# Where the low part of a weight tile is made: a VectorE subtraction, or an accumulating transfer onto a negated copy

## The chip, the cores and the metric

The kernel runs on one core of one Trainium2 chip. Its time is the device time of one execution in microseconds (us); the number that counts is the median of several runs. A profiled execution gives the trace that the views below are taken from.

## What is computed

A decoder trunk of one layer on 1024 positions of 1024 channels, in float32:

```
h  = layer_norm(x)
u  = h @ w_in                        # GLU | z | x,B,C | dt | gate_a | gate_b
ya = silu(layer_norm(conv31(a * sigmoid(g)))) @ w_conv_out
yb = rms_norm(ssd(silu(conv4(xBC)), dt) * silu(z)) @ w_ssm_out
h  = layer_norm(alpha*h + (sigmoid(gate_a)*ya + sigmoid(gate_b)*yb) @ w_o)
h  = layer_norm(alpha*h + (silu(gate) * val) @ w_down),  gate,val = conv3(h @ w_up)
```

`conv31`, `conv4` and `conv3` are causal depthwise convolutions along the positions, `ssd` the chunked Mamba-2 recurrence with 32 heads in 4 groups.

## The kernel before, in words

**Two parts per operand.** The big products are done in float32r, to which a float32 number is rounded. To keep accuracy each operand is held as two float32r parts: a high part, the rounded number, and a low part, what the rounding left. A product is then three matmuls, high by high, high by low and low by high (`mm3`, L158 to L163; the last, L163, is the first to read the low part of its first operand). Activations are split by `split_to`, `transpose_to`, `split_pair` and `parts`; weights by `weights` (L144 to L153), which the change touches.

**A weight tile.** `weights` loads 128 rows of 1024 float32 numbers (512 KB) from memory into a staging tile `st` (pool `wst`, 3 buffers) through SP's queue, L147. It then takes a tile `w` of two halves of 1024 from the pool `wsp` (3 buffers; the last two tiles of each `w_down` pass come from buffers of their own). ScalarE copies `st` into the high half and rounds in doing so (L149, shown as CAST). VectorE writes `st` minus the high half into the low half (L150). For the three tiles of `first_columns` in the first half, GpSimd does that subtraction (`eng=G`). All of it is issued at a raised priority (`high_priority(offset=4000)`), so that the scheduler places it early. 284 weight tiles go through this function.

**The stages.** The positions are worked in two halves of 512. For each half: `ln_in` (normalise, transpose to `hT`), `mixers` (the in-projection, column block by column block with `column`, `z_gate` and `glu`, 24 matmuls of 512 columns for each weight tile; among them the SSD of four groups, the convolutions, and from group 2 on the first half of the SSM out-projection), `combine` (gates, second half of the SSM out-projection, the conformer's layer norm and out-projection) and the out-projection by `w_o`. For the first half that is `out_proj`; for the second it is `out_proj_pairs`, which goes through the positions in two pairs of blocks, so that every one of its 16 weight tiles serves only 12 matmuls.

Then comes the FFN. `up_first` (one weight tile `w_ue`, 24 matmuls) runs for 8 blocks ahead and then between the blocks of `up_rest`, which makes three more split tiles for each block by `split_pair` (VectorE still subtracts there; two of the three, of 1024 columns, sit in `wsp` too). `down` goes through the 22 blocks of `w_down` twice, once for each half of the positions, 24 matmuls for each weight tile.

**What sets the order.** Each engine runs its instructions in one fixed order that the scheduler wrote; an instruction that waits for a semaphore holds up all that stand behind it on its engine. SP issues every transfer of the kernel before. GpSimd has little to do: a product `au` for every chunk of the SSD (L473), the sums for the mean and the variance in `combine` (L611 to L624), a few subtractions. VectorE carries the long convolution `conv31` (L415, 480 instructions at lowered priority, fitted in where there is room), the short one (L370), the SSD's elementwise work, and the splits.

A `w` buffer is free again when the last matmul of its old tile has run. Then the high half can be written, then the low half, and then the first L163 of the new tile can run.

Of the kernel before, what the change touches and what calls it, by code (L numbers as in the profile page):

```python
# [8 lines left out]
F32 = mybir.dt.float32  # L9
F32R = mybir.dt.float32r  # L10
AF = mybir.ActivationFunctionType
ALU = mybir.AluOpType
# [43 lines left out]
def kernel(  # L56
# [15 lines left out]
    V, A, G, TE, SY = nc.vector, nc.scalar, nc.gpsimd, nc.tensor, nc.sync  # L72
# [14 lines left out]
    def bank(which):  # L87
# [20 lines left out]
        out=head_of,  # L108
        in_=ident.rearrange("p (g k h) -> p g h k", k=4, h=8),
        axis=AX.X,  # L110
        op=ALU.add,
# [3 lines left out]
        out=kind, in_=ident.rearrange("p (g k h) -> p k g h", k=4, h=8), axis=AX.XY, op=ALU.add  # L115
# [28 lines left out]
    def weights(src, name, pl=None, eng=None, bufs=None):  # L144
        with tc.high_priority(offset=4000):
            st = wst.tile([P, D], F32, tag="st", name=f"st_{name}")
            SY.dma_start(st, src)  # L147
            w = (pl or wsp).tile([P, 2, D], F32R, tag="w", bufs=bufs, name=f"w_{name}")
            A.copy(w[:, 0, :], st)  # L149
            (eng or V).tensor_tensor(  # L150
                out=w[:, 1, :], in0=st, in1=w[:, 0, :].bitcast(F32), op=ALU.subtract
            )
        return w  # L153

    def big_tile(name):
# [182 lines left out]
    def column(hh, hT, ct):  # L338
        ps = bank(1)
        project(ps, weights(wcol[ct], f"c{hh}_{ct}"), hT)  # L340
        return ps

    def first_columns(hh, hT, cts):

        ws = [weights(wcol[ct], f"c{hh}_{ct}", eng=None if hh else G) for ct in cts]
        pss = [bank(1) for _ in cts]
        for q in range(2):
            ts = slice(q * 256, (q + 1) * 256)
            for w, ps in zip(ws, pss):
                for n, (i, j) in enumerate(((0, 0), (1, 0), (0, 1))):  # L350
                    for k in range(KD):
                        TE.matmul(  # L352
                            ps[:, ts],
                            w[:, i, k * P : (k + 1) * P],
                            hT[:, j, k, ts],
                            start=n == 0 and k == 0,
                            stop=n == 2 and k == KD - 1,
                        )
        return pss
# [23 lines left out]
    def glu(pl, hh, hT, i):  # L383
        pa, pg = bank(1), bank(1)
        wa = weights(wcol[CT_A + i], f"ga{hh}_{i}")
        project(pa, wa, hT)
        wg = weights(wcol[CT_G + i], f"gg{hh}_{i}")
        project(pg, wg, hT)
        v = pl.tile([P, HALF + KC - 1], F32, tag="v", bufs=4, name=f"v{hh}_{i}")
        s = pl.tile([P, HALF], F32, tag="sig", name=f"sig{hh}_{i}")  # L390
        A.activation(out=s, in_=pg, func=AF.Sigmoid)
        A.copy(v[:, : KC - 1], v_halo[:, i, :])
        V.tensor_mul(v[:, KC - 1 :], pa, s)
        if hh == 0:
            A.copy(v_halo[:, i, :], v[:, HALF:])
        return v
# [678 lines left out]
```

## Time and profile before

| | |
|---|---|
| median of 3 runs | 2039.45 us (2036.19 to 2040.29) |
| the profiled execution: device time | 2041.08 us |
| its span in the trace | 2039.3 us |
| TensorE (PE) busy | 2000.0 us, 98% |
| VectorE (DVE) busy | 1654.7 us, 81% |
| ScalarE (ACT) busy | 973.0 us, 48% |
| GpSimd (POOL) busy | 148.0 us, 7% |
| DMA queue of SP | 278.24 MB, 40.3% of the 16 engines' span |

How to read the views: "busy" is the time in which an engine ran at least one instruction. Matmuls overlap in the record (one lasts about 390 ns, the next starts after about 227), so that PE's pace is read from the starts, or from the count in a stretch, and not from the mean. The view of groups gives, for one line of the kernel and one shape, the count, the busy time, the mean of one in ns, and the idle time before them. The view of waits says which instruction stood idle for which other one. The view of windows gives the busy time and count of each engine in a stretch, then the granted TensorE clock, the mean busy share of the 16 DMA engines, and GB/s. In the list of transfers stand the count, the size of one, and the median time from issue to landing.

### The profile page before, as it was taken

How to read it: one execution, taken by the hardware profiler on the slowest of the kernel's cores; microseconds unless marked ns; L12 is line 12 of the kernel's file. 1: busy time of each engine (PE TensorE's matmuls, PEld its weight loads, DVE VectorE, ACT ScalarE, POOL GpSimd, SP SyncE). 2: the span in 40 equal slices, each digit the busy share in tenths (PEclk: the TensorE clock that was granted, in tenths of full speed). 3: DMA queues.
4: the chain of work that ended last, by engine and by line, in shares of the span. 5: the costliest groups of instructions: out<-in, count | busy, mean ns of one | idle time of the engine just before them, and what ended most of it. 6: DMA issues, size and time to landing. Idle time of an engine off the chain costs nothing.

```text
span 2039.3 us, 24778 instructions
## 1 busy us (share of the span) xinstructions
PE 2000.0 (98%) x9296; PEld 1650.1 (81%) x9296; DVE 1654.7 (81%) x2185; ACT 973.0 (48%) x1392; POOL 148.0 (7%) x125
## 2 busy tenths in 40 slices
PE   7999999999999999999999999999999999999998
PEld 6888887888788888888888888877888888888886
DVE  7599999989766869999998976586888888853736
ACT  4465654556453356665454635354444444433231
POOL 2010101001400000100100130010000000000000
PEclk9999999999999999999999999999999999999999
DMA  6222223333436522222323353566454444464542
GB/s 218 93 69 88 86 94 104 99 103 114 158 121 213 209 88 77 90 84 76 126 88 104 109 171 128 195 217 217 155 164 157 164 165 156 160 227 149 209 159 83
DMA packets 95015, 279.81 MB, mean 137 GB/s; under 512 B 10800, under 2 KB 10800, under 8 KB 94896
## 3 DMA queue, kind: packets, MB, share of 16 engines
q1 hardware_dynamic: 94896, 278.24, 40.3%
q8 instruction: 73, 1.20, 0.2%
q14 instruction: 46, 0.38, 0.1%
HBM read 229.96 MB, written 48.23 MB: 136 GB/s over the span
## 4 chain that ended last, share of the span: by engine, by line
PE 69%; DVE 23%; issue 4%; DMA 2%; ACT 1%; SPq 0%; POOL 0%; DVEq 0%; ACTq 0%
PE acc L163 15%; PE acc L161 15%; PE acc L162 15%; DVE c L415 8%; PE sm L161 6%; PE sm L163 6%; PE sm L162 6%; DVE xbc L370 2%; PE acc L352 1%; PE sm L529 1%; PE sm L510 1%; DVE w_so L150 1%; DVE w_z L150 1%; DVE w_c L150 1%; PE sm L187 1%
## 5 line engine op out<-in xcount | busy, mean ns | idle before, releaser
L415 DVE SCALAR_TENSOR_TENSOR c<-v,pc,c 128x512 f32<-128x512 f32 x480 | 375.3, 805 | 7.2 <-ACT c L404 5.8
L473 POOL TENSOR_TENSOR au<-seg_mv,head_of 128x1024 fp32r<-128x1024 f32 x32 | 77.6, 2425 | 961.8 <-PE sm L482 728.8
L161 PE MATMUL acc<-hT,w_c 128*128 128x512 f32 x352 | 141.0, 400 | 0.0
L162 PE MATMUL acc<-hT,w_c 128*128 128x512 f32 x352 | 140.6, 399 | 0.0
L163 PE MATMUL acc<-hT,w_c 128*128 128x512 f32 x352 | 138.4, 393 | 0.0
L150 DVE TENSOR_TENSOR w_dn<-st_dn,w_dn 128x1024 fp32r<-128x1024 f32 x44 | 53.4, 1222 | 104.2 <-ACT w_dn L149 104.2
L370 DVE SCALAR_TENSOR_TENSOR xbc<-u,pc,xbc 128x512 f32<-128x512 f32 x144 | 109.8, 774 | 0.7 <-ACT xbc L368 0.5
L161 PE MATMUL sm<-h1s,w_s 128*128 128x512 f32 x264 | 103.5, 392 | 6.0 <-DVE fuv L848 3.1
L149 ACT CAST w_dn<-st_dn 128x1024 fp32r<-128x1024 f32 x44 | 46.0, 1053 | 131.6 <-PE sm L163 115.4
L162 PE MATMUL sm<-h1s,w_s 128*128 128x512 f32 x264 | 102.8, 389 | 0.0
L163 PE MATMUL sm<-h1s,w_s 128*128 128x512 f32 x264 | 102.1, 389 | 0.0
L162 PE MATMUL acc<-w_z,hT 128*128 128x512 f32 x256 | 100.8, 394 | 0.0
L161 PE MATMUL acc<-w_z,hT 128*128 128x512 f32 x256 | 100.8, 401 | 0.0
L163 PE MATMUL acc<-w_z,hT 128*128 128x512 f32 x256 | 100.7, 396 | 0.0
L149 ACT CAST w_c<-st_c 128x1024 fp32r<-128x1024 f32 x50 | 52.5, 1051 | 86.9 <-PE acc L163 66.2
L162 PEld LDWEIGHTS acc<-hT,w_c 128*128 128x128 f32 x352 | 66.1, 188 | 16.9 <-issue 3.8
L163 PEld LDWEIGHTS acc<-hT,w_c 128*128 128x128 f32 x352 | 66.1, 188 | 16.1 <-issue 2.6
L161 PEld LDWEIGHTS acc<-hT,w_c 128*128 128x128 f32 x352 | 66.1, 188 | 15.9 <-issue 2.6
L150 DVE TENSOR_TENSOR w_c<-st_c,w_c 128x1024 fp32r<-128x1024 f32 x47 | 60.6, 1289 | 20.2 <-ACT w_c L149 20.2
L163 PE MATMUL acc<-h1b,w_ue 128*128 128x512 f32 x176 | 68.5, 391 | 2.0 <-DVE w_ue L150 2.0
L161 PE MATMUL acc<-h1b,w_ue 128*128 128x512 f32 x176 | 68.7, 391 | 1.1 <-ACT s L807 0.7
L163 PE MATMUL sm<-h1b,w_s 128*128 128x512 f32 x176 | 69.2, 393 | 0.0
(312 smaller groups left out, 5741.8 us busy)
## 6 DMA issues: line engine op xcount, KB each, us to landing
st_c<-wcol SPq DMA_DIRECT2D x50, 512.0 KB, 3.5
st_dn<-wdown SPq DMA_DIRECT2D x44, 512.0 KB, 3.6
st_z<-wz SPq DMA_DIRECT2D x32, 512.0 KB, 3.4
st_wo<-wo SPq DMA_DIRECT2D x24, 512.0 KB, 3.9
st_ue<-wup SPq DMA_DIRECT2D x22, 512.0 KB, 4.1
ra<-wup SPq DMA_DIRECT2D x22, 512.0 KB, 3.8
rb<-wup SPq DMA_DIRECT2D x22, 512.0 KB, 3.5
act_scr<-fo SPq DMA_DIRECT2D x22, 512.0 KB, 2.7
```

Source lines behind the costliest of these rows:

```text
L149: A.copy(w[:, 0, :], st)
L150: (eng or V).tensor_tensor(out=w[:, 1, :], in0=st, in1=w[:, 0, :].bitcast(F32), op=ALU.subtract)
L161: TE.matmul(ps, wa(0), xa(0), start=start, stop=False, skip_group_check=more)
L162: TE.matmul(ps, wa(0), xa(1), start=False, stop=False, skip_group_check=more)
L163: TE.matmul(ps, wa(1), xa(0), start=False, stop=stop, skip_group_check=more)
L187: TE.transpose(pt[:, i * P : (i + 1) * P], src[:, (q + i) * P : (q + i + 1) * P], ident)
L352: TE.matmul(ps[:, ts], w[:, i, k * P : (k + 1) * P], hT[:, j, k, ts], start=n == 0 and k == 0, stop=n == 2 and k == KD - 1,)
L370: V.scalar_tensor_tensor(out=o, in0=u[:, k : k + HALF], scalar=pc[:, wc + k : wc + k + 1], in1=o, op0=ALU.mult, op1=ALU.add,)
L415: V.scalar_tensor_tensor(out=accs[i], in0=v[:, k : k + HALF], scalar=pc[:, wc + k : wc + k + 1], in1=accs[i], op0=ALU.mult, op1=ALU.add,)
L473: G.tensor_tensor(out=au, in0=seg_mv[:, c, :].unsqueeze(1).to_broadcast([P, 8, P]), in1=head_of[:, g, :].unsqueeze(2).to_broadcast([P, 8, P]),
L510: TE.matmul(po, CT[:, cs], S, start=True, stop=True)
L529: TE.matmul(py[:, hs], m[:, h, :], xs[:, hs], start=True, stop=True)
```

## The change

The high half is made as before. The low half is first set to the negated high half by ScalarE; then a transfer issued by GpSimd reads the same 512 KB of weights from memory a second time and adds them to what stands there. VectorE (and, for the first three tiles, GpSimd) no longer subtracts. The argument `eng` of `weights` stays but is not used any more. `st` is now read by one instruction instead of two.

```diff
@@ weights(src, name, pl=None, eng=None, bufs=None) @@
             SY.dma_start(st, src)
             w = (pl or wsp).tile([P, 2, D], F32R, tag="w", bufs=bufs, name=f"w_{name}")
             A.copy(w[:, 0, :], st)
-            (eng or V).tensor_tensor(
-                out=w[:, 1, :], in0=st, in1=w[:, 0, :].bitcast(F32), op=ALU.subtract
-            )
+            A.activation(out=w[:, 1, :], in_=w[:, 0, :].bitcast(F32), func=AF.Copy, scale=-1.0)
+            G.dma_start(w[:, 1, :], src, accum_op=ALU.add)
         return w
```

## The prediction

> **What bounds the kernel now.** I read the page first (span, busy times, queues), then who TensorE waits for, then windows of single stages, and last the groups and transfers that the change touches.
>
> ```profile
> span 2039.3 us, 24778 instructions
> PE 2000.0 (98%) x9296; PEld 1650.1 (81%) x9296; DVE 1654.7 (81%) x2185; ACT 973.0 (48%) x1392; POOL 148.0 (7%) x125
> q1 hardware_dynamic: 94896, 278.24, 40.3%
> ```
>
> TensorE has only 2039.3 - 2000.0 = 39.3 us without work. That is an outer limit for any gain that leaves the matmuls alone. Who causes those gaps is in TensorE's own waits (us in total, times, longest):
>
> ```profile
> PE sm L187 <- DVE x L225: 13.1, 3, 12.0
> PE sm L161 <- DVE fuv L848: 3.1, 4, 0.8
> PE sm L161 <- ACT w_s L726: 2.9, 2, 2.7
> PE acc L162 <- DVE yT L194: 2.9, 1, 2.9
> PE acc L163 <- DVE w_ue L150: 2.0, 2, 1.1
> PE sm L482 <- DVE state L525: 1.4, 2, 0.9
> PE acc L161 <- ACT w_wo L149: 1.1, 1, 1.1
> ```
>
> The largest, 13.1, is the layer norm before the first matmul, which the change does not shorten. The waits for VectorE after that come to 3.1 + 2.9 + 2.0 + 1.4 = 9.4 us, and only 2.0 of them are for the subtraction that goes. So VectorE, 81% busy and often in the chain of waits, hardly ever lets TensorE stand; the weight tiles arrive in time.
>
> The windows show the margins by stage (busy and count of PE, PEld, DVE, ACT, POOL; clock; DMA share; GB/s): the start, mixers, the paired out-projection, the lead of the FFN, and down:
>
> ```profile
> 0.00:50.00 50.00, 37.16 (x229) 34.33 (x230) 38.85 (x64) 23.18 (x45) 10.85 (x15) 1.00 0.65 222
> 100.00:200.00 100.00, 100.00 (x482) 81.99 (x481) 99.38 (x136) 62.63 (x102) 9.41 (x4) 1.00 0.25 83
> 1305.00:1356.00 51.00, 49.89 (x244) 41.17 (x242) 35.33 (x44) 27.51 (x39) 1.84 (x1) 1.00 0.77 272
> 1360.00:1410.00 50.00, 44.39 (x199) 35.46 (x199) 39.30 (x53) 27.25 (x45) 7.70 (x8) 1.00 0.68 232
> 1800.00:1900.00 100.00, 100.00 (x443) 82.81 (x442) 42.17 (x47) 32.12 (x39) 0.00 (x0) 1.00 0.51 181
> ```
>
> In the last row 443 matmuls take 100 us: 0.226 us each, 5.42 us for a weight tile of 24, 2.71 for one of 12. In the mixers VectorE is full, and TensorE is full as well.
>
> **The change part by part.** For each of 284 tiles:
>
> ```profile
> L149 ACT CAST w_dn<-st_dn 128x1024 fp32r<-128x1024 f32 x44 | 46.0, 1053 | 131.6 <-PE sm L163 115.4 <-DMA st_dn<-wdown 16.3
> L150 DVE TENSOR_TENSOR w_dn<-st_dn,w_dn 128x1024 fp32r<-128x1024 f32 x44 | 53.4, 1222 | 104.2 <-ACT w_dn L149 104.2
> L859 ACT ACTIVATE fo<-fug,pc 128x1024 f32<-128x1024 f32 x22 | 25.2, 1145 | 0.0
> L473 POOL TENSOR_TENSOR au<-seg_mv,head_of 128x1024 fp32r<-128x1024 f32 x32 | 77.6, 2425 | 961.8 <-PE sm L482 728.8 <-DVE seg_mv L323 232.9
> st_c<-wcol SPq DMA_DIRECT2D x50, 512.0 KB, 3.5
> r<-h_scr SPq DMA_DIRECT2D x12, 512.0 KB, 9.3
> 1820.41 0.33 SPq L147 DMA_DIRECT2D st_dn<-wdown  x1
> ```
>
> *Removed:* 281 VectorE subtractions of 1.22 us, 343 us of VectorE (and three on GpSimd). For TensorE that is worth what TensorE waited: at most 9.4 us; I take 5.
>
> *Added on ScalarE:* 284 negations. The nearest row is a scaled ACTIVATE of the same shape, 1.15 us: 326 us, which takes ACT from 973 to about 1300 us (64%), in the mixers from 63 to about 83 (18 tiles in 100 us). ScalarE does not become the bound, but its queue gets dense: the casts now mostly find it idle, and then will sometimes stand behind a negation or an activation.
>
> *Added on GpSimd and the DMA engines:* 284 accumulating transfers. No row shows one, so I bound it. Issue: between 0.33 us (SP's issue of a plain load) and 2.43 (GpSimd's longest frequent instruction); I take the middle, 1.4. Landing: between 3.5 us (a plain load of the size) and 9.3 (the slowest plain one). An accumulation must also read the place that it adds to, so I take the nearest, 3.5, plus the time of another 512 KB: 278.24 MB in 40.3% of 2039.3 us is 339 GB/s, 1.55 us. Half of another 1.55 stands for meeting the next tile's plain load. Together 1.4 + 3.5 + 1.55 + 0.5 * 1.55 = 7.2; with some overlap of issue and transfer I use 6.9 (ends: 3.8 and 11.7).
>
> No row shows an adding transfer. The Trainium skill ("Collectives: The Full Stack", "The bandwidth ceiling: the fold count and why AG ≠ RS ≠ AR") says that a reducing transfer moves at half the rate of a copy, because both operands are read through the same ring. By it the transfer part is an estimated 3.1 us, which is what doubling gives too. With the plain row alone the sum below would be about 40 us less.
>
> *The chain that matters* runs from the last matmul of a buffer's old tile to the first L163 of its new one. Before: cast 1.05 and subtraction 1.22, 2.3 us. After: 1.05 + 1.15 + 6.9 = **9.1 us** (ends 6.0 and 13.9). Against it stands the window that three buffers give: two whole tiles and the two matmuls before the first L163, 50 matmuls, 11.3 us; in the paired out-projection 26 matmuls, 5.9. In the order of the changed program I counted the matmuls between each release and the first low read, following queues and semaphores: the mixers have a median near 12 us, down 11.1, but 16 tiles of the paired stage a median of 6.9, and of the 22 of up_first two have 5.9, eight 8.6, two 9.1 and the rest over 10. Of the others seven lie below 9.1 (5.1 to 8.6). The waits of GpSimd's `au` products for TensorE, ahead of some of the transfers in its queue, are in that count and cost these windows 1 us at most; in turn `au` now stands behind transfers, but it was made long ahead (row L473: 728.8 us spent on waiting for TensorE, not the reverse).
>
> *The sum, against the profiled 2041.1 us (span 2039.3 and 1.8 around it):*
>
> - Paired out-projection. Three tiles take one chain and the 10 matmuls left: (9.1 + 2.26) / 3 = 3.79 instead of 2.71 us, 16 tiles: +17. Its DMA share is 0.77 already. 272 GB/s at 0.77 is 353 at full; 13.9 MB in 51 us and 2 * 8.4 MB more need 87 us, +36, if the second read counts in full. Between the two: +25.
> - up_first: shortfalls 2 * 3.2 + 8 * 0.5 = 10.4 us; its lead runs at a DMA share of 0.68: +14.
> - Seven other short windows: shortfalls sum to 16 us, neighbours share: +10.
> - Mixers and combine, some 200 tiles with a margin of 2 to 3 us: a late cast (a table load 1.28 and an activation 0.7) uses it up; one in five late by 0.9 on TensorE after sharing is 36, of which a stall widens the next windows: +20.
> - Start, DMA share 0.65, three tiles at once and a fourth with a window of 5.1: +5.
> - Down: 181 GB/s at 0.51 is 355 at full; 181 + 2 * 96 = 374 would need 5% more than there is, of 2 * 22 * 5.42 = 238 us: 0 to 13; I take +8.
> - VectorE's relief: -5.
>
> 25 + 14 + 10 + 20 + 5 + 8 - 5 = +77: 2118. The profiled run is 1.6 over the median of 2039.45, so I forecast **2116 us**, 3.8% slower.
>
> In the mixers VectorE is busy 99.38 of 100 us. The Trainium skill ("SBUF — State Buffer", "SBUF: two separate sides") warns that a transfer issued by GpSimd can stand still while VectorE holds the port that they share, in its two-port modes; the instructions that fill VectorE here read two tensors, and for those the page names no block of descriptor writing. Were they to block, one L415 (0.8 us) ahead of each transfer would make the chain 9.9 and add some 20 us; no row can tell yet.
>
> **The rivals.**
>
> *It fits everywhere, and VectorE's relief is left.* With an issue of 0.33 and a landing of 3.5 the chain is 6.0; the paired stage then needs (6.0 + 2.26) / 3 = 2.75 against 2.71 us, and nothing stalls but two or three single tiles. TensorE gets back most of its 9.4 us of waits for VectorE: 2031. It decides below a transfer of about 4.2 us in all. For it: plain loads land in 3.5 us and SP issues them in 0.33. Against it: a second operand to read, an issue by software, and 149 MB more on the queues.
>
> *No difference.* A transfer of 4.5 to 5 us: the paired stage loses 5 us, VectorE gives as much back: 2036 to 2043.
>
> *The transfer is slow.* At 11.7 us (landing of the slowest plain row, issue of an `au`) the chain is 13.9. A regular tile then takes (13.9 + 4.97) / 3 = 6.29 instead of 5.42 us where the window is 11.3, and 0.57 us more where it is 12.2: 246 tiles, +140 to +214. The paired stage adds 16 * 2.68 = 43, up_first about 33, the start 10: 2265 to 2340. For it: the DMA share of 0.65 to 0.77 in three stages, and adding arithmetic that no row here bounds. Against it: in the mixers the queues are a quarter busy.
>
> *ScalarE becomes the bound* instead of the transfer: at 83% in the mixers, in one fixed order, it would hold PSUM evacuation back too. 100 us of mixers hold 63 + 21 of work; only waits inside the queue could lengthen it, by some 30 us over both halves: 2070 with a fast transfer. That is a part of my forecast's band.
>
> That VectorE still subtracts is excluded: in the changed program's order 281 of its instructions are gone.
>
> **How the numbers follow.** The forecast, 2050 to 2200 (a chain of about 8 to 11.5 us): 0.55. Slow transfer, over 2200: 0.23, most of it below 2340. Fits everywhere: 0.12. No difference: 0.10. A difference of 0.2%, 4 us, is about what a measurement of this kernel can tell from none. Faster 0.12, same 0.10, slower 0.78. The range runs from 2036, which leaves out most of the first rival, to 2340, the upper end of the third, with about 0.1 beyond each.
>
> **What would show it.** Right: VectorE at about 1310 us; ACT near 1300; TensorE's waits headed by L163 and L352 waiting for the transfers of w_wo, w_ue and single w_c, with the paired stage stretched from 51 to about 75 us and down almost unchanged; a DMA share well over 0.8 in the paired stage; an issue-to-landing time of 5 to 6 us for the transfers of GpSimd and about 1.4 for their issue. Wrong: gaps before nearly every tile's first L163 (the slow transfer); no such waits at all (it fits); or waits of TensorE for ScalarE's PSUM copies (ScalarE bound). If accumulation costs the DMA engines no second read, the terms for the paired stage, the lead and down shrink by about half.

## The result and the profile after

The changed kernel takes **2159.2 us** (2157.28 to 2164.62, 4 runs) against 2039.8 us before (4 runs): a ratio of 1.0594, 95% interval 1.057 to 1.0618. It is slower by 119 us. The forecast was 2116, 43 us less, and the band that it stood for 2050 to 2200.

First the head of the page of the changed kernel, to be held against the one before:

```profile
span 2155.9 us, 25135 instructions
PE 2035.4 (94%) x9296; PEld 1662.2 (77%) x9296; DVE 1346.1 (62%) x1904; ACT 1256.7 (58%) x1683; POOL 362.6 (17%) x406
q0 software_dynamic: 40896, 148.92, 40.2%
q1 hardware_dynamic: 94896, 278.24, 37.3%
```

VectorE lost 309 us of work, and TensorE does the same 9296 matmuls in 117 us more. Of these, 81 us are idle time (2155.9 - 2035.4 = 120.5 against 39.3 before). The other 35 us are busy time, 2035.4 against 2000.0: the same matmuls run more slowly. The granted clock is 0.979 over the span, against 0.996 before; by an estimate from these numbers, 0.021 * 2155.9 - 0.004 * 2039.3 = 37 us of full clock are missing. The new queue moves 148.92 MB in 40.2% of the span, 172 GB/s; the plain one 278.24 MB in 37.3%, 346 GB/s. Taken by the byte, an adding transfer holds the DMA engines twice as long.

Who TensorE waits for (us in total, times, longest):

```profile
PE acc L161 <- DMA w_wo<-wo: 18.4, 9, 3.2
PE acc L161 <- DMA w_dn<-wdown: 17.9, 6, 8.4
PE sm L186 <- DVE x L224: 17.0, 2, 12.6
PE acc L162 <- DMA w_ue<-wup: 12.2, 9, 3.9
PE acc L162 <- DMA w_gb<-wcol: 11.5, 4, 6.8
PE acc L162 <- DMA w_sp<-wssm: 9.2, 2, 5.8
PE acc L160 <- ACT w_gb L149: 4.3, 2, 2.3
PE sm L743 <- DMA r<-h_scr: 3.5, 1, 3.5
```

Where before the list was headed by a layer norm and then fell to 3 us, there are now five rows of TensorE waiting for a weight tile's low part, 69 us together. L162 is the L163 of before. Where the weight tile is the second operand (w_wo, w_dn, w_z), its low part is read one matmul earlier, by L161. The new steps themselves, in the groups and in the list of transfers (here the last number is the median from issue to landing):

```profile
L150 ACT ACTIVATE w_dn<-w_dn 128x1024 fp32r<-128x1024 f32 x44 | 46.5, 1057 | 0.2
L151 POOL DMA_DIRECT2D w_c<-wcol x50 | 43.4, 868 | 246.3 <-ACT w_c L150 157.8
w_c<-wcol POOLq DMA_DIRECT2D x50, 512.0 KB, 6.5
w_dn<-wdown POOLq DMA_DIRECT2D x44, 512.0 KB, 7.9
w_wo<-wo POOLq DMA_DIRECT2D x24, 512.0 KB, 8.2
```

The negation takes 1.06 us, the issue by GpSimd 0.87, and the transfer lands 5.7 (w_z) to 8.2 us after its issue begins, so that these times hold the 0.87. From cast to landing that is 7.8 to 10.3 us when nothing stands between the steps, where the prediction had 9.1. Single tiles take longer: of the 16 in the paired stage, read one by one in the trace, 9.1 to 14.1 us, with a median of 11.3.

The stages, from the start of the first matmul on one kind of weight tile to that on the next (us; "first half" from the span's start to the first w_gt, "mixers 2" from the second half's first w_c to w_gt, "combine" both halves from w_gb to w_co, "w_o 1" from the first w_wo to the next half's first matmul on w_c, "paired" from the second half's first w_wo to w_ue, "up" from there to the first w_dn, "down" to the end). What lies between them, from w_gt to w_gb and from w_co to w_wo, changes by less than 1 us. The column "idle" says how much of the difference is idle time of TensorE; the last is the prediction's term, whose "seven other short windows" are not given a place there:

| stage | before | after | difference | idle | predicted |
|---|---|---|---|---|---|
| first half | 441.2 | 451.3 | +10.1 | +5.1 | start +5, mixers and combine +20, |
| mixers 2 | 422.5 | 428.6 | +6.1 | +3.6 | other short windows +10 |
| combine | 191.7 | 215.3 | +23.6 | +20.8 | (in the three above) |
| w_o 1 | 49.1 | 60.0 | +10.9 | +7.8 | none |
| paired | 51.0 | 79.0 | +28.0 | +18.8 | +25 |
| up | 428.7 | 441.6 | +12.9 | +5.5 | +14 |
| down | 254.1 | 279.6 | +25.5 | +19.6 | +8 |

### The profile page after: what moved, and what is told of

Read it like the earlier page. It is cut to its first block, busy times and chain, and to the rows that moved or that the text cites. A ratio compares the mean times of both kernels' runs of the same rounds, so it can differ in the third digit from the quotient of the medians.

```text
span 2155.9 us, 25135 instructions
## 1 busy us (share of the span) xinstructions
PE 2035.4 (94%) x9296; PEld 1662.2 (77%) x9296; DVE 1346.1 (62%) x1904; ACT 1256.7 (58%) x1683; POOL 362.6 (17%) x406
## 3 DMA queue, kind: packets, MB, share of 16 engines
q0 software_dynamic: 40896, 148.92, 40.2%
q1 hardware_dynamic: 94896, 278.24, 37.3%
## 5 line engine op out<-in xcount | busy, mean ns | idle before, releaser
L414 DVE SCALAR_TENSOR_TENSOR c<-v,pc,c 128x512 f32<-128x512 f32 x480 | 380.0, 815 | 12.7 <-ACT c L403 8.1
L162 PE MATMUL acc<-hT,w_c 128*128 128x512 f32 x352 | 139.8, 398 | 2.2 <-DMA w_c<-wcol 2.2
L726 DVE TENSOR_TENSOR w_act<-ar,w_act 128x512 fp32r<-128x512 f32 x44 | 30.2, 691 | 174.5 <-ACT w_act L725 174.5
L161 PE MATMUL acc<-hT,w_c 128*128 128x512 f32 x352 | 138.8, 394 | 0.0
L161 PE MATMUL acc<-w_z,hT 128*128 128x512 f32 x256 | 102.3, 400 | 3.3 <-DMA w_z<-wz 3.3
L161 PE MATMUL sm<-h1s,w_s 128*128 128x512 f32 x264 | 102.7, 389 | 0.0
L162 PE MATMUL sm<-h1s,w_s 128*128 128x512 f32 x264 | 101.7, 390 | 0.0
L162 PE MATMUL acc<-w_z,hT 128*128 128x512 f32 x256 | 101.0, 396 | 0.0
L161 PE MATMUL acc<-w_dn,w_act 128*128 128x512 f32 x176 | 70.4, 400 | 18.0 <-DMA w_dn<-wdown 17.9
L472 POOL TENSOR_TENSOR au<-seg_mv,head_of 128x1024 fp32r<-128x1024 f32 x32 | 68.2, 2130 | 102.2 <-PE sm L481 90.6
L151 POOL DMA_DIRECT2D w_c<-wcol x50 | 43.4, 868 | 246.3 <-ACT w_c L150 157.8
L162 PE MATMUL acc<-h1b,w_ue 128*128 128x512 f32 x176 | 71.1, 407 | 12.3 <-DMA w_ue<-wup 12.2
L162 PEld LDWEIGHTS acc<-hT,w_c 128*128 128x128 f32 x352 | 66.1, 188 | 20.6 <-DMA w_c<-wcol 5.3
L596 DVE TENSOR_TENSOR mb<-yb,acc 128x512 f32<-128x512 f32 x16 | 10.9, 680 | 109.3 <-PE acc L162 85.8
L161 PEld LDWEIGHTS acc<-hT,w_c 128*128 128x128 f32 x352 | 66.1, 188 | 16.4 <-issue 3.1
```

What stands on the lines that cost most here:

```text
L151: G.dma_start(w[:, 1, :], src, accum_op=ALU.add)
L161: TE.matmul(ps, wa(0), xa(1), start=False, stop=False, skip_group_check=more)
L162: TE.matmul(ps, wa(1), xa(0), start=False, stop=stop, skip_group_check=more)
L414: V.scalar_tensor_tensor(out=accs[i], in0=v[:, k : k + HALF], scalar=pc[:, wc + k : wc + k + 1], in1=accs[i], op0=ALU.mult, op1=ALU.add,)
L472: G.tensor_tensor(out=au, in0=seg_mv[:, c, :].unsqueeze(1).to_broadcast([P, 8, P]), in1=head_of[:, g, :].unsqueeze(2).to_broadcast([P, 8, P]),
L596: V.tensor_add(m, ya, ps)
```

## The experiments

**Theory 1**: a weight tile's low part is late wherever its chain (cast, negation, transfer) is longer than the window that three buffers give, and the transfer is the long piece of it, because of its bytes and their double reading. **Rivals**: ScalarE's extra work; a fixed price of any transfer from GpSimd; the traffic as such; DMA engines that are full. The stage times of all runs but `load`, `mixlate` and `mixneg` stand in one table after the experiments.

### negonly: the negation without the transfer

```diff
             A.activation(out=w[:, 1, :], in_=w[:, 0, :].bitcast(F32), func=AF.Copy, scale=-1.0)
-            G.dma_start(w[:, 1, :], src, accum_op=ALU.add)
+            (eng or V).tensor_tensor(
+                out=w[:, 1, :], in0=st, in1=w[:, 1, :].bitcast(F32), op=ALU.add
+            )
```

> The negation on ScalarE stays, and VectorE adds the staged tile to it: the transfer alone is taken away. Theory 1 (the transfer comes too late): the chain is 1.05 + 1.05 + 1.22 = 3.3 us, under every window, so 2035 to 2052. Rival (ScalarE's 284 negations delay its casts and PSUM copies): half or more of the loss stays, 2090 to 2150.

Measured 2068.66 us, ratio 1.0143 (1.0125 to 1.0162). This is neither of the two: the negation alone costs 29 us as long as VectorE still has its full load. These 29 us cannot be added to the transfer's, though: see `tiny`, which has the negations and a small transfer and no addition on VectorE.

### plain: a copy in place of the addition

```diff
-            G.dma_start(w[:, 1, :], src, accum_op=ALU.add)
+            G.dma_start(w[:, 1, :], src)
```

> The changed kernel with a plain copy by GpSimd's queue in place of the adding one; the low part is then the whole weight, so that the product is not the reference's. It moves the same 149 MB, with the same issue, wait and negation, but reads no second operand. Theory 1a (the adding transfer holds the DMA engines twice as long): about 5 us to landing instead of 6.5, and two thirds of the loss goes, 2055 to 2085. Rival 1b (any transfer from GpSimd is too long a chain, whatever it does): 2120 to 2160.

Measured 2093.41 us, ratio 1.0265 (1.0245 to 1.0284). From the page and the list of transfers of this run:

```profile
q0 software_dynamic: 40896, 148.92, 22.4%
w_c<-wcol POOLq DMA_DIRECT2D x50, 512.0 KB, 3.8
w_wo<-wo POOLq DMA_DIRECT2D x24, 512.0 KB, 6.0
L151 POOL DMA_DIRECT2D w_dn<-wdown x44 | 23.3, 530 | 225.0 <-ACT w_dn L150 225.0
```

The same packets and bytes take 22.4% of 2092.1 us, 318 GB/s, against 172 when they add: 1.85 times as fast. The two kinds shown land 2.7 and 2.2 us sooner, all kinds 1.5 to 2.8. The issue is not the same, as the expectation had it: a copy takes GpSimd 0.53 us, an adding transfer 0.87. So 66 of the 119 us belong to the addition, its longer issue and its longer landing together. The rest, 53 us, is more than theory 1a had foreseen by its band and less than 1b.

### mixonly and restonly: the change in a part of the stages

```diff
+            if name[0] in "cgzs" and name[:2] not in ("gb", "sp", "co"):     # mixonly; restonly has it reversed
                 A.activation(out=w[:, 1, :], in_=w[:, 0, :].bitcast(F32), func=AF.Copy, scale=-1.0)
                 G.dma_start(w[:, 1, :], src, accum_op=ALU.add)
+            else:
+                (eng or V).tensor_tensor(
+                    out=w[:, 1, :], in0=st, in1=w[:, 0, :].bitcast(F32), op=ALU.subtract
+                )
```

> The adding transfer for the 146 tiles of the mixers (windows of about 12 us) alone, VectorE's subtraction for the other 138 (combine, both out-projections by w_o, up_first, down). Theory 1 (only short windows and full DMA engines cost): 2040 to 2055, the rest being the start. Rival 2 (each transfer costs alike): 146 of 284 of the loss, about 2100.

> The reverse: the adding transfer for the 138 tiles of combine, the out-projections by w_o, up_first and down; VectorE's subtraction in the mixers. Theory 1: nearly the whole loss, 2135 to 2160. Rival 2 (each transfer costs alike): about 2098.

Measured 2046.21 us, ratio 1.0026 (1.0016 to 1.0035), and 2143.76 us, ratio 1.0508 (1.0487 to 1.053). 146 transfers in the mixers cost 6 us, 138 in the other stages 103. The small cost is a balance: in the profiled run of `mixonly` the first half and the second half's mixers lose 9.1 and 2.4 us, and combine, where VectorE still subtracts, gains 9.5. Transfers do not cost alike; where they stand decides.

### tiny: the same chain almost without bytes

```diff
-            G.dma_start(w[:, 1, :], src, accum_op=ALU.add)
+            G.dma_start(w[:, 1, :16], src[:, :16], accum_op=ALU.add)
```

> The changed kernel with an adding transfer of 16 of the 1024 columns; the rest of the low part stays the negated high part, so that the product is not the reference's. Negation, issue and wait stay, the bytes go. If the fixed part of the chain is what costs: within 20 us of the changed kernel, about 2140. If the time grows with the bytes (landing and full DMA engines): near the run with the negation alone, 2065 to 2085, with the paired stage (51.0 us before, 79.0 changed) at 55 to 60.

Measured 2049.53 us, ratio 1.0038 (1.0025 to 1.0052): below the lower of the two forecasts. From this run's list of transfers (8 KB are 128 rows of 16 numbers):

```profile
w_c<-wcol POOLq DMA_DIRECT2D x50, 8.0 KB, 2.4
w_dn<-wdown POOLq DMA_DIRECT2D x44, 8.0 KB, 3.4
```

284 negations, 284 issues and 284 waits cost 8 us in all, with VectorE's relief already taken off. What the change costs comes with the bytes: 44 us when they are copied, another 66 when they are added.

### halfload: a quarter of a megabyte less of plain load for each tile

```diff
-            st = wst.tile([P, D], F32, tag="st", name=f"st_{name}")
-            SY.dma_start(st, src)
+            st = wst.tile([P, HALF], F32, tag="st", name=f"st_{name}")
+            SY.dma_start(st, src[:, :HALF])
...
-            A.copy(w[:, 0, :], st)
+            A.copy(
+                w[:, 0, :].rearrange("p (r n) -> p r n", r=2),
+                st.unsqueeze(1).to_broadcast([P, 2, HALF]),
+            )
```

> The changed kernel with half of the plain load: 512 columns of each weight tile go to the staging tile and are cast into both halves of the high part, so that the product is not the reference's. Casts, negations, adding transfers and waits stay; a quarter of a megabyte less moves for each tile. If full DMA engines set the loss in the paired stage and in down (a tile there costs them 3 and 3.5 units of 512 KB, the adding one counted as two; now 2.5 and 3): the paired stage goes from 79 to about 66, down from 280 to 262 to 266, 2159 to about 2125. If only the chain's length counts: 2150 or more, as the landing shortens by less than 1 us.

(The high part of the second 512 columns is that of other weights here; the low part takes up the difference, so that the two still sum to the weight.) Measured 2168.77 us, ratio 1.0634 (1.0604 to 1.0665): no gain, on the contrary. The paired stage takes 79.0 us, as in the changed kernel, at a DMA share of 0.92 instead of 0.99, and down takes 275.5. The windows of this run over down, and over up (last two numbers: DMA share, GB/s):

```profile
2000.00:2100.00 100.00, 93.93 (x396) 76.10 (x395) 32.80 (x57) 43.41 (x55) 14.67 (x17) 0.97 0.85 216
1600.00:1700.00 100.00, 90.52 (x376) 73.27 (x377) 68.04 (x79) 40.20 (x44) 3.51 (x13) 0.95 0.50 153
```

In the changed kernel the same stretches read:

```profile
2000.00:2100.00 100.00, 96.85 (x425) 79.27 (x424) 33.54 (x58) 43.91 (x55) 13.00 (x16) 1.00 0.97 267
1600.00:1700.00 100.00, 99.77 (x438) 81.71 (x437) 85.19 (x100) 46.35 (x50) 4.69 (x16) 1.00 0.60 179
```

With the share down from 0.97 to 0.85, TensorE is no faster. In these two stages the loss does not follow the bytes that the DMA engines carry. And up became 30 us longer at a share of 0.50. The scheduler placed the tiles of up_first otherwise. Counted in matmuls from the release of the buffer to the first low read, at 0.227 us each, 10 of the 22 windows are under 9 us in the changed kernel and 16 in this one; the medians are 9.1 and 8.6. TensorE's waits there:

```profile
PE acc L165 <- DMA w_ue<-wup: 34.4, 14, 5.1
```

The changed kernel has 9 such waits of 12.2 us. That is the same transfer, landing a little sooner (6.5 us against 7.3), in shorter windows: the clearest sight of the mechanism in these runs, and it was not planned.

### negfirst: the negation ahead of the cast

```diff
-            A.copy(w[:, 0, :], st)
-            A.activation(out=w[:, 1, :], in_=w[:, 0, :].bitcast(F32), func=AF.Copy, scale=-1.0)
+            A.activation(out=w[:, 1, :], in_=st, func=AF.Copy, scale=-1.0)
             G.dma_start(w[:, 1, :], src, accum_op=ALU.add)
+            A.copy(w[:, 0, :], st)
```

> The changed kernel with the negation taken from the staged tile and put ahead of the cast, so that the transfer starts one ScalarE instruction (1.05 us) sooner; the same result, the same traffic. By the theory of the chain: about 1 us less for every tile that is late (some 60 to 80 of them), 2090 to 2125, most of it in combine and up_first. If full DMA engines set all of it: 2150 to 2160.

Measured 2149.89 us, ratio 1.0531 (1.0515 to 1.0547): the forecast of 2090 to 2125 missed, and the total lies at the edge of what full DMA engines would give, 2150 to 2160. The stages do not bear that reading out, because they move both ways. Combine falls as expected, to 195.6 us from 215.3, and w_o 1 falls to 54.3 from 60.0. But up takes 469.6, with a shift of the order as in `halfload` (20 of the 22 windows under 9 us, w_ue waited for 15 times), and the paired stage stays at 78.6. The transfers of this run suggest why a microsecond in the chain is not a microsecond gained:

```profile
st_wo<-wo SPq DMA_DIRECT2D x24, 512.0 KB, 7.9
w_wo<-wo POOLq DMA_DIRECT2D x24, 512.0 KB, 8.6
```

With the cast first, the staging buffer comes free at the cast's end, and the next plain load has a start of a negation and an issue over the adding transfer: they landed after 5.0 and 8.2 us. Here both start together and land after 7.9 and 8.6.

### wxcomb: two more buffers in the second combine

```diff
+            if extra and pl is None:
+                n_x[0] += 1
+                pl = extra[0] if n_x[0] % 5 in (2, 4) else None
             w = (pl or wsp).tile([P, 2, D], F32R, tag="w", bufs=bufs, name=f"w_{name}")
...
     state_stack.close()
+    wx_stack = ExitStack()
+    extra.append(wx_stack.enter_context(tc.tile_pool(name="wx", bufs=2)))
     mixT = combine(1, hT, yT)
+    extra.clear()
+    wx_stack.close()
```

> The changed kernel with two more buffers for the weight tiles of the second half's combine (five in rotation, where the space of the SSD's states has come free). From the first w_gb to the first w_co there: 91.4 us before, 103.0 changed. Theory 1a (a chain longer than its window): 91 to 94, and about 2149 in all. Rival 4 (the DMA engines are full there, share 0.84 to 0.98): over 100, about 2159.

Measured 2154.9 us, ratio 1.0552 (1.0536 to 1.0568); from w_gb to w_co 102.4 us. That is what rival 4 had forecast: the window alone is not what fails here. The timelines of this run (start, length, instruction, and in brackets the idle time before it) show the longest of the waits there:

```profile
1239.62 1.05 ACT L154 CAST w_sp<-st_sp 128x1024 fp32r<-128x1024 f32 x1 [14.04 <-DMA st_sp<-wssm]
1241.66 1.03 ACT L154 CAST w_gb<-st_gb 128x1024 fp32r<-128x1024 f32 x1
1244.09 0.86 POOL L156 DMA_DIRECT2D w_gb<-wcol  x1 [1.16 <-ACT w_gb L155]
1253.04 0.80 PE L167 MATMUL acc<-hT,w_gb 128*128 128x512 f32 x1 [6.05 <-DMA w_gb<-wcol]
```

ScalarE stands 14 us for the plain load of w_sp, which lands 15.4 us after its issue, at a DMA share of 0.93 (1195 to 1250 us). The cast of a w_gb whose own load had landed more than 15 us before stands behind it in ScalarE's queue, and TensorE waits 6.05 us for that tile. So here the traffic does cost, by way of a late plain load; with a quarter of a megabyte less for each tile (`halfload`), combine still took its 215.3 us.

In the changed kernel the waits of combine come from other queues of fixed order. In the first half a transfer whose negation was done at 531.85 stands behind six of GpSimd's sums for the mean, and TensorE waits 6.82 us for it:

```profile
526.61 8.46 POOL L612 TENSOR_TENSOR mean<-mean,cc 128x512 f32<-128x512 f32 x6
535.01 0.87 POOL L151 DMA_DIRECT2D w_gb<-wcol  x1
543.55 0.79 PE L162 MATMUL acc<-hT,w_gb 128*128 128x512 f32 x1 [6.82 <-DMA w_gb<-wcol]
```

In the second half a negation stands 7 us behind its own cast in ScalarE's queue:

```profile
1267.91 1.04 ACT L149 CAST w_sp<-st_sp 128x1024 fp32r<-128x1024 f32 x1
1275.85 1.05 ACT L150 ACTIVATE w_sp<-w_sp 128x1024 fp32r<-128x1024 f32 x1
1277.19 0.86 POOL L151 DMA_DIRECT2D w_sp<-wssm  x1 [14.02 <-ACT w_sp L150]
```

### vneg: the negation on VectorE

```diff
-            A.activation(out=w[:, 1, :], in_=w[:, 0, :].bitcast(F32), func=AF.Copy, scale=-1.0)
+            V.tensor_scalar_mul(w[:, 1, :], w[:, 0, :].bitcast(F32), -1.0)
```

> The changed kernel with the negation on VectorE in place of ScalarE: ScalarE's queue is that of before, the transfer stays. If the negation on ScalarE cost its 29 us beside the transfer (the sum of two causes): about 2130. If both only lengthen one chain, of which the transfer is the larger part: 2145 to 2165.

Measured 2149.04 us, ratio 1.0528 (1.0501 to 1.0555). Taking the negations off ScalarE gives 10 us in all, not 29. That fits one chain of which the negation is the small part, but the run does not separate it cleanly: VectorE now has the work. The mixers of the second half lose 12 us against the changed kernel and up 7, while the paired stage gains 5 and down 9. A negation of w_c, w_z or w_dn takes VectorE 0.69 us, so that the chain is also 0.4 us shorter there.

### load: the traffic without anyone waiting for it

```diff
+    sc = [dram.tile([P, D + 16], F32, name=f"sc{i}")[:, :D] for i in range(4)]
+    n_sc = [0]
+    for i in range(4):
+        SY.dma_start(sc[i], wdown[i])
...
             (eng or V).tensor_tensor(
                 out=w[:, 1, :], in0=st, in1=w[:, 0, :].bitcast(F32), op=ALU.subtract
             )
+            n_sc[0] += 1
+            G.dma_start(sc[n_sc[0] % 4], src, accum_op=ALU.add)
```

> The kernel before, with 284 more adding transfers of the same weights by GpSimd's queue into scratch memory that nobody reads: the traffic without anything that waits for it (four loads of 512 KB at the start set the scratch). Theory 1 (the low part is late because its own chain is long): 2040 to 2060. Rival 3 (the traffic delays the plain loads, whoever waits for the sums): 2080 to 2120.

Measured 2296.75 us, ratio 1.1249 (1.1232 to 1.1266), outside both. The run does not answer its question. All the transfers were issued early, the last at 904 us; that nothing asked for the sums is the likely reason. The DMA share is 0.9 or more in the first 16 of 40 slices and near that of before in the rest, and the transfers into memory landed after 11 to 14 us. GpSimd's queue was blocked, and with it the products of the SSD:

```profile
PE sm L489 <- POOL au L480: 147.9, 12, 32.8
```

### mixlate and mixneg: a version that might win

```diff
+            mixer = name[0] in "cgzs" and name[:2] not in ("gb", "sp", "co")
+            if mixer and name.split("_")[0] + name.split("_")[1] not in (
+                "c040", "c032", "c036", "c140", "c132", "c136", "c016", "c017", "c116"):
                 A.activation(out=w[:, 1, :], in_=w[:, 0, :].bitcast(F32), func=AF.Copy, scale=-1.0)
                 G.dma_start(w[:, 1, :], src, accum_op=ALU.add)
+            else:
+                (eng or V).tensor_tensor(
+                    out=w[:, 1, :], in0=st, in1=w[:, 0, :].bitcast(F32), op=ALU.subtract
+                )
```

(`mixneg` has the same condition and the order of `negfirst`.)

> The version that the runs point to: the adding transfer for the tiles of the mixers alone, without the first tiles of each half (w_c 40, 32, 36, and 16 and 17), VectorE's subtraction for all others. The one with them took 8 us longer up to its first gate tile, and 10 less in the first combine. Expected 2028 to 2038; if the relief of VectorE was only a chance of the order, 2038 to 2046.

> The version with the adding transfer in the mixers alone, without the first tiles, and with the negation ahead of the cast. The mixers lost 4 us a half in the version with the cast ahead, and the first combine gained 9. Expected 2030 to 2040; a clear gain over the kernel before needs the mixers' loss to go.

Measured 2040.25 us, ratio 0.9993 (0.9984 to 1.0001), and 2041.37 us, ratio 1.0002 (0.9993 to 1.0011): no difference. By the forecast of `mixlate`, 2040 means that VectorE's relief was only a chance of the order. Combine does take less, 182.3 and 181.7 us instead of 191.7, and a part of that can be seen. Before, TensorE waits there 2.85 us for VectorE (L194) and 0.83 for ScalarE, and then its matmuls start 0.427 us apart for 6 us instead of 0.227; neither wait stands in the two versions. The two mixers lose about as much, 4 and 5 us in the first of the two versions, 8 and 2 in the second.

### All stages

| us | before | after | tiny | negonly | plain | mixonly | restonly | halfload | negfirst | wxcomb | vneg |
|---|---|---|---|---|---|---|---|---|---|---|---|
| first half | 441.2 | 451.3 | 440.5 | 447.2 | 444.3 | 450.3 | 442.9 | 451.1 | 452.4 | 452.4 | 452.6 |
| mixers 2 | 422.5 | 428.6 | 420.4 | 426.8 | 427.0 | 424.9 | 422.8 | 424.8 | 428.0 | 428.5 | 440.3 |
| combine | 191.7 | 215.3 | 192.0 | 202.0 | 203.2 | 182.2 | 214.4 | 215.3 | 195.6 | 211.0 | 214.1 |
| w_o 1 | 49.1 | 60.0 | 48.8 | 50.1 | 56.2 | 49.3 | 59.3 | 53.9 | 54.3 | 59.9 | 60.6 |
| paired | 51.0 | 79.0 | 58.0 | 55.3 | 67.2 | 50.3 | 78.7 | 79.0 | 78.6 | 74.3 | 74.0 |
| up | 428.7 | 441.6 | 430.2 | 426.4 | 428.8 | 428.3 | 441.8 | 471.8 | 469.6 | 443.9 | 449.0 |
| down | 254.1 | 279.6 | 254.1 | 255.0 | 265.0 | 254.1 | 281.8 | 275.5 | 270.8 | 276.3 | 270.5 |

## Why the prediction came out as it did

**Right.** TensorE was the bound and had nothing to win: `mixlate` gains 9 us in one stage and loses them in others. The sign and the mechanism hold: the waits are for the transfers. They stand at w_wo and w_ue, as named, and also at w_gb, w_sp and w_dn, which the prediction did not name, while w_c, which it named, has only 5.6 us. The chain of 9.1 us lies inside the measured 7.8 to 10.3, partly by luck. Issue and landing together were put at 6.9 us, and the median of the 284 transfers is 6.7; in it the issue is 0.87 and not 1.4, and the rest 5.8 and not 5.5.

**The size: +77 forecast, +117 in the profiled runs.** The 40 us that are missing are mainly down (17.5), the first out-projection (10.9), and the relief of 5 that did not show in the total. The prediction also counted in waits alone. TensorE's slower matmuls, 35 of the 117 us, are no term of it. Right after the longest wait, 8.4 us, the matmuls start 0.427 us apart for 3 us, at a granted clock of 0.51, and then 0.227 again.

**Paired stage: +25, measured +28, near by luck.** The prediction took a mean of the chain's +17 and of the full engines' +36. `halfload` speaks against full engines: a quarter of a megabyte less for each tile left 79.0 us. The chain was put too short, at 9.1 us where the tiles of this stage have a median of 11.3. With that its own formula gives (11.3 + 2.26) / 3 = 4.52 us for a tile, 16 * 1.81 = 29 us. The trace divides the stage's loss otherwise: eight waits for w_wo of 16.9 us in all and one of 3.5 us for r, which lands late, with 1.5 us idle before, and 9 us of slower matmuls at a granted clock of 0.87. The traffic counts, but as a longer landing (6.0 us for a copy, 8.2 adding), not as a rate.

**Up: +14, measured +12.9**, and sensitive to the order: with 16 or 20 windows under 9 us in place of 10 it is +41 to +43.

**Mixers, combine, start and other short windows: +35, measured +40**, with a wrong division. The mixers with their windows of 12 us were nearly free (`mixonly`, 2 to 9 us a half with the start), and combine took 24. There it is not the window alone: a negation stands behind other work of ScalarE, a transfer behind the sums, in queues of fixed order. The prediction had counted such a delay as one late cast in five; in combine it came as eight waits of 25 us in all, the longest 6.8.

**Down: +8, measured +25.5.** The step that failed is "down almost unchanged". Its term was a shortage of DMA rate, 0 to 13 us; `halfload` at a share of 0.85 still needs 275.5. What the trace shows are six waits for w_dn, 17.9 us in all, and 6 us of slower matmuls. Two of the waits, 2.2 and 8.4 us, fall at the passage from up to down. In the order of the changed program the first three tiles of w_down have windows of 6.8, 5.9 and 8.6 us, so that a part of the prediction's +10 for short windows belongs here, and their casts, negations and other work of ScalarE stand in one queue:

```profile
1890.70 0.86 POOL L151 DMA_DIRECT2D w_dn<-wdown  x1 [16.25 <-ACT w_dn L150]
1894.57 0.86 POOL L151 DMA_DIRECT2D w_dn<-wdown  x1 [3.01 <-ACT w_dn L150]
1896.56 0.86 POOL L151 DMA_DIRECT2D w_dn<-wdown  x1 [1.12 <-ACT w_dn L150]
1900.07 0.79 PE L161 MATMUL acc<-w_dn,w_act 128*128 128x512 f32 x1 [8.43 <-DMA w_dn<-wdown]
```

The other four waits, 7.3 us together, are spread over the rest of the stage, and between them the chain, 1.05 + 1.06 + 7.9 = 10.0 us by the means, does fit the windows of 11.1. Why these four tiles were late was not tested.

**The first out-projection: no term, measured +10.9.** `restonly` has it, `mixonly` has not. There the view of windows shows a DMA share of 0.97 (600 to 700 us), and the loads of x land after 8.8 us in place of 6.7 (median of both halves). TensorE waits 7.6 us there for the layer norm of the second half's x, against 0.7 before, and 1.6 for a w_wo: mostly a delay of plain loads, which the prediction's terms did not know.

**VectorE's relief: -5.** In the changed kernel's list the waits for yT (2.9 us), w_ue (2.0) and state (1.4) are gone, as forecast; what that is worth in time cannot be told apart. **ScalarE as the bound** did not come: 1257 us, 58%. `negonly` (+29) beside `tiny` (+8) suggests that the negations cost most when VectorE has to follow them with its own full queue; by which instruction stays open.

**Rate and port.** The Trainium skill ("Collectives: The Full Stack", "The bandwidth ceiling: the fold count and why AG ≠ RS ≠ AR") says of collectives that reducing halves the rate of a copy. Here the rates on the same queue are 172 and 318 GB/s, a factor of 1.85, which agrees in size. The Trainium skill ("SBUF — State Buffer", "SBUF: two separate sides") ties the blocked transfers to VectorE's two-port modes and names no block of descriptor writing for instructions that read two tensors. The trace agrees: an issue takes 868 ns in the mixers (w_c), where VectorE is about 90% busy, and 870 in the paired stage, where it is a third.

## What to carry to other kernels

Before an operation is moved from a half-idle engine to a transfer, compare the new chain from buffer release to first use with the window that the buffers give, stage by stage; engine totals said nothing here, and 138 tiles with short windows or dense queues cost 103 us where 146 with 12 us cost 6. An adding transfer has to be reckoned at nearly twice a copy of the DMA engines' time, here 1.85. A chain in several queues of fixed order can be held up at each of them, and two more buffers did not help against that in `wxcomb`. Waits cost more than their length: a third of the loss here is matmuls that run more slowly, at a lower granted clock.

## What the runs showed of the hardware

- An adding transfer of 512 KB lands 5.7 to 8.2 us after GpSimd begins to issue it, a copy of the same size on the same queue 3.8 to 6.0, an adding one of 16 columns (8 KB) 2.2 to 4.4 (medians by kind of tile). The issue takes 0.87 us when it adds, with 1024 columns as with 16, and 0.53 us when it copies.
- Where the changed kernel makes TensorE wait, its granted clock is lower: 0.87 from 1355 to 1435 us, the paired stage, 0.979 over the whole, against 0.996 before.

```profile
1355.00:1435.00 80.00, 59.68 (x236) 46.45 (x235) 26.77 (x39) 45.72 (x59) 18.00 (x19) 0.87 0.99 272
```
